# One kernel for two transformer blocks: the output gates' linears move into the recurrences, the modulation weights get a tile of their own in the expert phase

## The chip, the cores and the metric

The kernel runs as one program on 1 core of one Trainium2 chip. The metric is the device time of one execution in microseconds (us). The core's engines are called as in the profile: PE (matrix multiplication), PEld (PE's weight load), DVE (vector), ACT (activations), POOL, and SP, which here only starts DMA transfers.

## What is computed

256 tokens of 1024 channels pass through two blocks, batch 1, everything in fp32.

- Block 1: an adaptive norm (shift, scale and gate of each sub-layer come from `silu(c) @ w_mod + b_mod`), a mixer and a SwiGLU feed-forward. The mixer runs the gated recurrence HGRN2 forward and backward in 4 heads of 128, sums them, and gates: `o_a = rmsnorm(o_f + flip(o_b), g_norm_a) * silu(og)` with `og` one of the columns of the input projection. A second branch is a gated MLP over positions (`u`, `v`); both are merged.
- Block 2, layer 0: chunked gated linear attention (GLA: 4 heads, keys of 128, values of 256, chunks of 64), `o = rmsnorm(o, norm_g) * silu(og)`, then `w_out`. Layer 1: sliding window attention. Behind each stands PEER: a product-key lookup picks 16 of 16384 experts for each of 8 heads of each token, and the experts' `u` and `v` rows are applied. Both layers have their own modulation, and so have the shared keys and values (kv).

## The kernel before

**Linears.** A linear is fp32 made of three matmuls of a reduced 32-bit type (high x high, low x high, high x low: `mm3`, lines 276 to 280). Weights come in halves of 128x1024 (512 KB). For each half, `halves` (lines 257 to 266) starts a DMA on SP's queue into the ring `raw` (line 219; 4 buffers, and more of them, shown as `rawx`, where a stage has room), ACT rounds it to `wh` (line 262), DVE takes the rest as `wl` (line 264; rings of 3 and extras), and PE runs 12 matmuls of 128x512 on it. After each half `pump` adds `s.rate` to a credit, and each full credit calls the background work once.

**Background work: the modulations.** `w_mod` is 1024 x 1024 for each part. A piece (an eighth, 512 KB) is DMAed through the same `raw` ring and multiplied into the activated condition row by one DVE `scalar_tensor_tensor` with a sum (`mod_part`, line 374), which writes over the piece. After eight pieces the part is done (line 378). Where a part is wanted, `need` does what is left at once. Rates: 0.2 in block 1's recurrences, 0.6 from the gates on and in the feed-forward, 0.4 in GLA; in layer 0's PEER 0 in the U phase, 0.45 in the first 36 pairs of the V phase, 0.75 after; in layer 1's V phase 0, then 0.2.

**The order of instructions.** The program is written as one stream, and a scheduler gives each engine its list: it takes what it expects to be ready, in the order of the program where several are. On the chip each engine keeps its list in order and waits for semaphores. Where the scheduler's expectation of a time is off, an engine waits in front of work that is ready.

**The stages that the change touches.**
- Block 1, lines 700 to 875: for `d` in (0, 1) the forget gates f (lines 749 to 753), the products, transposes (L771) and the recurrence. After both: `on`, the sum of squares, `ro`; then the linears og (`w_in` 4, lines 860 to 862, Silu out of PSUM), gu and gv; then `on` times `ro` (L870), times the norm's weights (L872), times og (L873), three passes of 128x512 for each half of the tokens. The transposes of the result are L563.
- GLA, lines 1095 to 1190: q and k linears, k's decayed copy `kd` (L1116, L1117), the transposes of it (L1123), scores, states, outputs (`po` to `on`, line 1172), sums of squares (L1174, L1175), `ro`; then two linears for og (L1181), then the three passes of 128x1024 (L1184, L1186, L1187).
- Feed-forward, lines 960 to 1000: `up0` finishes the first up-block (its transposes are L974), then for each i `up(i + 1)` and the down-projection of block i.
- PEER's `route`, lines 1447 to 1459: the first query linear comes in token-major form; ACT copies it (L1452), PE transposes it (L1455), then the other three query linears run.
- PEER's V phase, lines 1678 to 1735: for each of 64 pairs two halves of `peer_v`, each with 12 matmuls, summed into 4 PSUM banks that stay open. The tile `RO` (1 buffer, 4 KB a partition) serves the gate groups before (line 1630) and the first pair's weights `W01` in this phase; after it, nothing until the next layer.

## Time and profile before

| | |
|---|---|
| median of 3 runs | 2375.7 us (2370.49 to 2376.27) |
| the profiled execution | 2370.87 us, of it the span 2369.1 us |
| mean granted clock of PE | 0.992 of full speed |
| PE busy | 2302.0 us of the span, 97% |
| DVE, ACT busy | 1846.0 us (78%), 1174.3 us (50%) |
| DMA | 475.97 MB, mean 201 GB/s |

The span is the time from the first to the last instruction of the profiled execution; 1.8 us lie around it. An entry such as "idle 2.41 <-DVE w L1117" says that the engine stood still for 2.41 us and that the DVE instruction of line 1117 ended that. Line numbers are those of the kernel before.

### The profile page before, as it was taken

The page shows a single profiled execution, that of the slowest core. Times are in us where ns is not written, and L with a number is a line of the kernel's source. Part 1 is how long each engine was busy: PE and PEld are TensorE (multiplying, and loading weights), DVE is VectorE, ACT ScalarE, POOL GpSimd, SP SyncE. Part 2 cuts the span into 40 slices and gives each one's busy share as a digit, 9 for nine tenths or more (in the row PEclk, how much of TensorE's full clock was granted, in tenths as well). Part 3 has the DMA queues.
Part 4 walks back from the last instruction along what each step waited for, and adds up shares of the span by engine and source line. Part 5 has one row for each costly group of instructions (what it writes and reads, how often), then busy time and mean ns, then how long its engine had stood idle before and what let it go on. Part 6 is the DMA issues. An engine that isn't in the chain of part 4 may idle for free. (4 is left out here: it accounts for less than half of the span.)

```text
span 2369.1 us, 39891 instructions
## 1 busy us (share of the span) xinstructions
PE 2302.0 (97%) x15360; PEld 2043.0 (86%) x15360; DVE 1846.0 (78%) x3502; ACT 1174.3 (50%) x1897; POOL 16.3 (1%) x32
## 2 busy tenths in 40 slices
PE   8999999999999999999999999999999999999998
PEld 6989889976899999997777887589999999888886
DVE  5589887778589989997677877659997999556665
ACT  4464454464445544445454556555454445445543
POOL 0000000000000000000000000000000000000000
PEclk9999999999999999999999999999999999999999
DMA  8537599655445544447778984154554445656773
GB/s 303 177 110 276 174 358 367 219 180 183 144 165 188 162 159 154 150 162 257 252 263 291 346 312 161 45 171 161 179 169 159 153 153 170 189 189 216 240 233 97
DMA packets 130590, 475.97 MB, mean 201 GB/s; under 512 B 15056, under 2 KB 15824, under 8 KB 129120
## 3 DMA queue, kind: packets, MB, share of 16 engines
q1 hardware_dynamic: 130208, 473.41, 59.0%
q8 instruction: 120, 1.97, 0.3%
q14 instruction: 70, 0.57, 0.1%
q0 software_dynamic: 192, 0.02, 0.0%
HBM read 472.30 MB, written 1.07 MB: 200 GB/s over the span
## 5 line engine op out<-in xcount | busy, mean ns | idle before, releaser
L264 DVE TENSOR_TENSOR wl<-raw,wh 128x1024 fp32r<-128x1024 f32 x425 | 517.7, 1221 | 136.7 <-ACT wh L262 135.3
L262 ACT ACTIVATE wh<-raw 128x1024 fp32r<-128x1024 f32 x425 | 448.4, 1056 | 342.9 <-issue 114.3
L1603 PE MATMUL psB<-acth,wh 128*128 128x256 f32 x1776 | 503.6, 284 | 1.6 <-ACT u L1609 1.6
L1605 PE MATMUL psB<-acth,wl 128*128 128x256 f32 x1776 | 500.0, 282 | 0.0
L1604 PE MATMUL psB<-actl,wh 128*128 128x256 f32 x1776 | 499.6, 281 | 0.0
L279 PE MATMUL psA<-wl,acth 128*128 128x512 f32 x880 | 351.3, 399 | 10.7 <-DVE wl L264 10.5
L278 PE MATMUL psA<-wh,acth 128*128 128x512 f32 x880 | 349.9, 398 | 3.5 <-ACT acth L551 2.3
L280 PE MATMUL psA<-wh,actl 128*128 128x512 f32 x880 | 349.2, 397 | 0.5 <-DVE actl L552 0.5
L1603 PEld LDWEIGHTS psB<-acth,wh 128*128 128x128 f32 x1776 | 334.6, 188 | 2.0 <-ACT u L1609 2.0
L1605 PEld LDWEIGHTS psB<-acth,wl 128*128 128x128 f32 x1776 | 334.6, 188 | 0.3 <-DVE wl L264 0.3
L1604 PEld LDWEIGHTS psB<-actl,wh 128*128 128x128 f32 x1776 | 334.7, 188 | 0.0
L279 PEld LDWEIGHTS psA<-wl,acth 128*128 128x128 f32 x880 | 165.9, 189 | 56.2 <-DVE wl L264 16.9
L1697 ACT ACTIVATE acth<-u 128x256 fp32r<-128x256 f32 x240 | 98.5, 416 | 223.1 <-PE psA L279 222.4
L278 PEld LDWEIGHTS psA<-wh,acth 128*128 128x128 f32 x880 | 165.8, 189 | 44.4 <-ACT acth L551 2.4
L280 PEld LDWEIGHTS psA<-wh,actl 128*128 128x128 f32 x880 | 165.6, 188 | 41.0 <-DVE actl L552 0.9
L264 DVE TENSOR_TENSOR wlx<-raw,whx 128x1024 fp32r<-128x1024 f32 x116 | 140.9, 1221 | 38.5 <-ACT whx L262 38.2
L262 ACT ACTIVATE whx<-raw 128x1024 fp32r<-128x1024 f32 x116 | 121.3, 1055 | 74.3 <-PE psB L1604 30.2
L1698 DVE TENSOR_TENSOR actl<-u,acth 128x256 fp32r<-128x256 f32 x240 | 99.7, 422 | 64.3 <-ACT acth L1697 64.3
L262 ACT ACTIVATE wh<-rawx 128x1024 fp32r<-128x1024 f32 x95 | 100.3, 1059 | 86.5 <-PE psB L1604 42.8
L264 DVE TENSOR_TENSOR wl<-rawx,wh 128x1024 fp32r<-128x1024 f32 x95 | 115.9, 1222 | 28.5 <-ACT wh L262 28.0
L262 ACT ACTIVATE whx<-rawx 128x1024 fp32r<-128x1024 f32 x86 | 90.5, 1058 | 83.8 <-PE psB L1604 14.2
L374 DVE SCALAR_TENSOR_TENSOR raw<-raw,L 128x1024 f32<-128x1024 f32 x61 | 74.7, 1224 | 60.7 <-DMA raw<-in_w_kv 30.1
(557 smaller groups left out, 4599.4 us busy)
## 6 DMA issues: line engine op xcount, KB each, us to landing
raw<-in_peer_u SPq DMA_DIRECT2D x212, 512.0 KB, 3.9
raw<-in_peer_v SPq DMA_DIRECT2D x209, 512.0 KB, 4.8
raw<-in_w_m SPq DMA_DIRECT2D x83, 512.0 KB, 5.4
rawx<-in_peer_v SPq DMA_DIRECT2D x47, 512.0 KB, 5.9
rawx<-in_w_m SPq DMA_DIRECT2D x45, 512.0 KB, 6.8
rawx<-in_peer_u SPq DMA_DIRECT2D x44, 512.0 KB, 3.8
raw<-in_w_in SPq DMA_DIRECT2D x27, 512.0 KB, 4.8
rawx<-in_w_up SPq DMA_DIRECT2D x25, 512.0 KB, 8.9
```

Source lines behind the costliest of these rows:

```text
L262: s.queue(nc.scalar.activation(wh, x, AF.Copy))
L264: s.queue(nc.vector.tensor_tensor(wl, x, wh.bitcast(F32), op=OP.subtract))
L278: mm(out, lhsT=lh, rhs=rh, start=start, stop=False)
L279: mm(out, lhsT=lh, rhs=rl, start=False, stop=False)
L280: mm(out, lhsT=ll, rhs=rh, start=False, stop=stop)
L374: s.queue(nc.vector.scalar_tensor_tensor(r, r, 1.0, s.crow, op0=OP.mult, op1=OP.mult, accum_out=m[:, k:k + 1]), 0)
L1603: mm(pu, lhsT=wh[:, sl], rhs=hT[:, k], start=(k == 0), stop=False)
L1604: mm(pu, lhsT=wh[:, sl], rhs=lT[:, k], start=False, stop=False)
L1605: mm(pu, lhsT=wl[:, sl], rhs=hT[:, k], start=False, stop=(k == 7))
L1697: nc.scalar.activation(Wh, W, AF.Copy)
L1698: nc.vector.tensor_tensor(Wl, W, Wh.bitcast(F32), op=OP.subtract)
```

## The change

- The modulation's generator becomes three functions, and while `s.mraw_at` is set, the next piece is DMAed into one tile with the tag `RO` as soon as the piece before is multiplied, instead of through `raw` when its turn comes. It is set in the first 36 pairs of PEER's V phase; of the two layers only layer 0 has pieces there.
- Block 1's og linear moves into the first recurrence (d == 0), behind f, and is kept raw; later ACT makes its Silu in SBUF, and DVE multiplies the norm's weights into it. The three passes become one `scalar_tensor_tensor` per head (8 of 128x128).
- GLA's first og linear moves between `kd` and its transposes, the second stays behind the recurrence; the norm's weights are multiplied into og. The squares are taken by ACT out of PSUM with a sum (8 of 128x256), `rstd` runs for each half of the tokens, and the three passes become 8 `scalar_tensor_tensor` of 128x256.
- Feed-forward: `up(1)` is written ahead of `up0`, and the up-blocks run two ahead of the down-blocks.
- PEER's route: the transposes of the first query linear are written behind the second query linear.

```diff
@@ -157,6 +157,7 @@
+        s.mraw_at = None
...
@@ -179,7 +180,7 @@
-        s.ckey = None
+        s.ckey = s.mnext = None
...
@@ -353,28 +354,43 @@
             nc.vector.tensor_tensor(s.mods["m", part][:, kk * 2:kk * 2 + 2], pt,
                                     b.unsqueeze(2).to_broadcast([128, 2, 2]), op=OP.add)

-    def mod_part(s, key, part):
-
-
-        nc = s.nc
+    def mod_row(s, key):
+
         if s.ckey != (key == "m"):
             s.ckey = key == "m"
             s.crow = s.t(s.crow_at[0], [128, 1024], tag=s.crow_at[1], bufs=1)
             r = 0 if s.ckey else 1
-            nc.sync.dma_start(s.crow, s.a["crow"][r:r + 1, :].to_broadcast([128, 1024]))
-            nc.scalar.activation(s.crow, s.crow, AF.Silu)
-        w = s.a["w_" + key]
+            s.nc.sync.dma_start(s.crow, s.a["crow"][r:r + 1, :].to_broadcast([128, 1024]))
+            s.nc.scalar.activation(s.crow, s.crow, AF.Silu)
+
+    def mod_fetch(s):
+
+        if s.bg and s.mnext is None and s.mraw_at:
+            key, part, k = s.bg[0]
+            s.mnext = s.t(s.mraw_at[0], [128, 1024], tag=s.mraw_at[1], bufs=1)
+            s.nc.sync.dma_start(s.mnext, s.a["w_" + key][part - s.part0[key], k])
+
+    def mod_piece(s):
+
+
+        nc = s.nc
+        key, part, k = s.bg[0]
         gate = part in (2, 5)
-        if gate:
-            m = s.t(s.small, [128, 8], tag="mgate", bufs=2)
-        else:
-            m = s.t(s.early if key == "m" else s.consts, [128, 8])
-        for k in range(8):
-            r = s.raw(w[part - s.part0[key], k])
-            s.queue(nc.vector.scalar_tensor_tensor(r, r, 1.0, s.crow, op0=OP.mult, op1=OP.mult,
-                                                   accum_out=m[:, k:k + 1]), 0)
-            if k < 7:
-                yield
+        s.mod_row(key)
+        s.mod_fetch()
+        r = s.raw(s.a["w_" + key][part - s.part0[key], k]) if s.mnext is None else s.mnext
+        s.mnext = None
+        s.bg.pop(0)
+        if k == 0:
+            if gate:
+                s.mcol = s.t(s.small, [128, 8], tag="mgate", bufs=2)
+            else:
+                s.mcol = s.t(s.early if key == "m" else s.consts, [128, 8])
+        m = s.mcol
+        s.queue(nc.vector.scalar_tensor_tensor(r, r, 1.0, s.crow, op0=OP.mult, op1=OP.mult, accum_out=m[:, k:k + 1]), 0)
+        s.mod_fetch()
+        if k < 7:
+            return
         nc.vector.tensor_tensor(m, m, s.col("mb", 8 * (s.modb0[key] + part), 8), op=OP.add)
         if gate:
             s.uid += 1
@@ -384,19 +400,15 @@
         else:
             s.mods[key, part] = m
         s.done.add((key, part))
-        yield

     def add_mods(s, key, parts):
         for p in parts:
-            s.bg.append(s.mod_part(key, p))
+            s.bg += [(key, p, k) for k in range(8)]

     def pump_n(s, n):
         while n > 0 and s.bg:
-            try:
-                next(s.bg[0])
-                n -= 1
-            except StopIteration:
-                s.bg.pop(0)
+            s.mod_piece()
+            n -= 1

     def pump(s):
         s.credit = getattr(s, "credit", 0.0) + getattr(s, "rate", 0.0)
@@ -708,6 +720,7 @@
                 s.more_mods()
             pb = s.pool("b1b", 1, ctx=c1)
             on = s.t(pb, [128, 2, 4, 128])
+            og = s.t(pb, [128, 2, 512])
             c2 = ExitStack()
             p = s.pool("b1a", 1, ctx=c2)
             w4 = lambda *sh: s.t(p, sh or [128, 4, 256], tag="w4", bufs=8)
@@ -751,6 +764,9 @@
                     nc.scalar.activation(f[:, :, h], bank, AF.Sigmoid)
                     nc.vector.tensor_scalar(f[:, :, h], f[:, :, h], lb1[:, d * 4 + h:d * 4 + h + 1],
                                             lb[:, d * 4 + h:d * 4 + h + 1], op0=OP.mult, op1=OP.add)
+                if d == 0:
+                    for b, y in enumerate(s.lin_nat(w_in, 4, hx, [0, 128])):
+                        nc.scalar.activation(og[:, b], y, AF.Copy)
                 kx, kc = w4(), w4()
                 nc.vector.tensor_scalar(kc, f[:, 1], -1.0, 1.0, op0=OP.mult, op1=OP.add)
                 nc.vector.tensor_scalar(kx, f[:, 0], -1.0, 1.0, op0=OP.mult, op1=OP.add)
@@ -857,20 +873,20 @@
             ro = s.rstd(pb, oss, 8, 128)
             s.rate = s.m2_rate

-            og = s.t(pb, [128, 2, 512])
-            for b, y in enumerate(s.lin_nat(w_in, 4, hx, [0, 128])):
-                nc.scalar.activation(og[:, b], y, AF.Silu)
+            for b in range(2):
+                nc.scalar.activation(og[:, b], og[:, b], AF.Silu)
+                o4 = og[:, b].rearrange("p (h e) -> p h e", h=4)
+                nc.vector.tensor_tensor(o4, o4, gna[:, None, :].to_broadcast([128, 4, 128]), op=OP.mult)
             gu = s.t(pb, [128, 2, 512])
             gv = s.t(pb, [128, 2, 512])
             for n, dst in ((5, gu), (6, gv)):
                 for b, y in enumerate(s.lin_nat(w_in, n, hx, [0, 128])):
                     nc.scalar.activation(dst[:, b], y, AF.Gelu_apprx_tanh)
             for b in range(2):
-                ov = on[:, b]
-                nc.vector.tensor_tensor(ov, ov, ro[:, 4 * b:4 * b + 4].unsqueeze(2).to_broadcast([128, 4, 128]),
-                                        op=OP.mult)
-                nc.vector.tensor_tensor(ov, ov, gna[:, None, :].to_broadcast([128, 4, 128]), op=OP.mult)
-                nc.vector.tensor_tensor(og[:, b], fl(ov), og[:, b], op=OP.mult)
+                for h in range(4):
+                    oh = og[:, b, h * 128:h * 128 + 128]
+                    nc.vector.scalar_tensor_tensor(oh, on[:, b, h], ro[:, 4 * b + h:4 * b + h + 1], oh, op0=OP.mult,
+                                                   op1=OP.mult)
             c2.close()
             p = s.pool("b1c", 1, ctx=c1)
             s.more(c1, 3, 6)
@@ -980,10 +996,12 @@
                 s.mm3(acc[b][n], z[0][:, h, bs], z[1][:, h, bs], w[0][:, sl], w[1][:, sl],
                       i == 0 and h == 0, i == 10 and h == 1)

-            zs = [up0()]
+            z1 = up(1)
+            zs = [up0(), z1]
             acc = [[s.ps("A", [128, 512]) for _ in range(2)] for _ in range(2)]
             for i in range(8):
-                zs.append(up(i + 1))
+                if i < 7:
+                    zs.append(up(i + 2))
                 for h, w in enumerate(s.halves(a["w_down"][i])):
                     for b in range(2):
                         for n in range(2):
@@ -1116,6 +1134,18 @@
                 nc.vector.tensor_tensor(kt[:, sl], bank, e2[:, sl], op=OP.mult)
                 last = nc.vector.tensor_tensor(kd[:, sl], bank, e3[:, sl], op=OP.mult)
             s.hold(last, 2, 2)
+            gn = s.row_bc(pb, "gla_norm")
+            og = s.t(pb, [128, 2, 1024])
+
+            def out_gate(n):
+
+                for b, y in enumerate(s.lin_nat(w, 4 + n, act, [0, 128])):
+                    o = og[:, b, n * 512:n * 512 + 512]
+                    nc.scalar.activation(o, y, AF.Silu)
+                    o2 = o.rearrange("p (h e) -> p h e", h=2)
+                    nc.vector.tensor_tensor(o2, o2, gn[:, None, :].to_broadcast([128, 2, 256]), op=OP.mult)
+
+            out_gate(0)
             kn = w4(128, 2, 4, 128)
             for b in range(2):
                 pt = s.ps("B", [128, 4, 128])
@@ -1152,6 +1182,7 @@
                                                 dv.unsqueeze(2).to_broadcast([128, 2, 256]), op=OP.mult)
                         nc.vector.tensor_tensor(so, pd, so, op=OP.add)
                 st[ch + 1] = sn
+            ros = []
             for b in range(2):
                 for i in range(2):
                     po = s.ps("C", [128, 2, 256])
@@ -1170,21 +1201,15 @@
                                 nc.tensor.matmul(po[64 * r:64 * r + 64, j], lhsT=qt[:, h, ch * 64:ch * 64 + 64],
                                                  rhs=st[ch][:, h], start=False, stop=(j == 1))
                     nc.scalar.activation(on[:, b, 2 * i:2 * i + 2], po, AF.Copy)
-                sq = w4()
-                nc.vector.tensor_tensor(sq, on[:, b], on[:, b], op=OP.mult)
-                nc.vector.tensor_reduce(oss[:, 4 * b:4 * b + 4], sq, axis=AX.X, op=OP.add)
-            ro = s.rstd(pb, oss, 8, 256)
-            gn = s.row_bc(pb, "gla_norm")
-            og = s.t(pb, [128, 2, 1024])
-            for n in range(2):
-                for b, y in enumerate(s.lin_nat(w, 4 + n, act, [0, 128])):
-                    nc.scalar.activation(og[:, b, n * 512:n * 512 + 512], y, AF.Silu)
+                    for j in range(2):
+                        h = 4 * b + 2 * i + j
+                        nc.scalar.activation(po[:, j], po[:, j], AF.Square, accum_out=oss[:, h:h + 1])
+                ros.append(s.rstd(pb, oss[:, 4 * b:4 * b + 4], 4, 256))
+            out_gate(1)
             for b in range(2):
-                ov = on[:, b]
-                nc.vector.tensor_tensor(ov, ov, ro[:, 4 * b:4 * b + 4].unsqueeze(2).to_broadcast([128, 4, 256]),
-                                        op=OP.mult)
-                nc.vector.tensor_tensor(ov, ov, gn[:, None, :].to_broadcast([128, 4, 256]), op=OP.mult)
-                nc.vector.tensor_tensor(og[:, b], fl(ov), og[:, b], op=OP.mult)
+                for h in range(4):
+                    oh = og[:, b, h * 256:h * 256 + 256]
+                    nc.vector.scalar_tensor_tensor(oh, on[:, b, h], ros[b][:, h:h + 1], oh, op0=OP.mult, op1=OP.mult)
             c2.close()
             p = s.pool("glac", 1, ctx=c1)
             s.more(c1, 3, 7)
@@ -1447,16 +1472,19 @@
         i50 = s.t(rp, [128, 50, 16], F16)
         nc.gpsimd.iota(i50, pattern=[[1, 50], [0, 16]], base=0, channel_multiplier=0,
                        allow_small_or_imprecise_dtypes=True)
-        for b, y in enumerate(qfirst):
-            q0 = s.t(rp, [128, 512], tag="sb", bufs=3)
-            nc.scalar.activation(q0, y, AF.Copy)
-            pt = s.ps("A", [128, 4, 128])
-            for j in range(4):
-                nc.tensor.transpose(pt[:, j], q0[:, j * 128:j * 128 + 128], s.ident)
-            nc.scalar.activation(qT[:, 0:4, b * 128:b * 128 + 128], pt, AF.Copy)
+        q0 = []
+        for y in qfirst:
+            q0.append(s.t(rp, [128, 512], tag="sb", bufs=3))
+            nc.scalar.activation(q0[-1], y, AF.Copy)
         for n in range(1, 4):
             for i, bank in enumerate(s.lin_T(a["peer_q"][l], n, act)):
                 nc.scalar.activation(qT[:, 4 * n + 2 * i:4 * n + 2 * i + 2], bank, AF.Copy)
+            if n == 1:
+                for b in range(2):
+                    pt = s.ps("A", [128, 4, 128])
+                    for j in range(4):
+                        nc.tensor.transpose(pt[:, j], q0[b][:, j * 128:j * 128 + 128], s.ident)
+                    nc.scalar.activation(qT[:, 0:4, b * 128:b * 128 + 128], pt, AF.Copy)
         yield
         for b in range(2):
             v16 = s.t(rp, [128, 16, 16], tag="v16", bufs=1)
@@ -1680,6 +1708,7 @@
             acc = [[s.ps("A", [128, 512]) for _ in range(2)] for _ in range(2)]
             W01 = s.t(rl, [128, 2, 2, 256], F32R, tag="RO", bufs=1)
             s.crow_at, s.ckey = (rl, "L"), None
+            s.mraw_at = rl, "RO"
             WH, WL = s.act_tiles()

             made = {}
@@ -1721,6 +1750,7 @@
                     kvp = s.pool("kv", 1, side="right", ctx=s.kvctx) if after == "swa" else None
                     vp = s.pool("peerv", 1, side="right", ctx=vc)
                     s.rate = s.v_rate
+                    s.mraw_at = None
                     s.more(vc, 2, 2, side="right")
                 if at == 58:
                     s.rate = 0.0
```

## Rows read from the trace of the kernel before

**Rows 1.** The page, part 1 (busy time, share, instructions) and lines of part 5.
```profile
PE 2302.0 (97%) x15360; PEld 2043.0 (86%) x15360; DVE 1846.0 (78%) x3502; ACT 1174.3 (50%) x1897; POOL 16.3 (1%) x32
...
L264 DVE TENSOR_TENSOR wl<-raw,wh 128x1024 fp32r<-128x1024 f32 x425 | 517.7, 1221 | 136.7 <-ACT wh L262 135.3
```

**Rows 2.** What the matmuls waited for, whole span: us in total, times, longest.
```profile
PE psA L279 <- DVE wl L264: 10.5, 10, 2.1
...
PE psB L771 <- DVE w L766: 4.2, 1, 4.2
...
PE psB L974 <- DVE z L972: 2.9, 2, 1.5
PE psB L1123 <- DVE w L1117: 2.4, 1, 2.4
```

**Rows 3.** Busy time by stretch: layer 0's V phase, then layer 1's.
```profile
core 0: us, PE busy (x) PEld busy (x) DVE busy (x) ACT busy (x) POOL busy (x), PEclk, DMA share, GB/s
1100.00:1270.00 170.00, 161.01 (x673) 125.81 (x671) 120.53 (x187) 81.31 (x119) 0.88 (x2) 0.99 0.78 260
2000.00:2170.00 170.00, 169.45 (x731) 136.14 (x730) 103.35 (x134) 89.38 (x139) 0.00 (x0) 1.00 0.62 199
```

**Rows 4.** Groups of 1075 to 1290 us: busy, mean ns, idle before and releasers.
```profile
L264 DVE TENSOR_TENSOR wl<-raw,wh 128x1024 fp32r<-128x1024 f32 x70 | 85.5, 1221 | 9.1 <-ACT wh L262 8.6
L262 ACT ACTIVATE wh<-raw 128x1024 fp32r<-128x1024 f32 x70 | 73.9, 1056 | 54.9 <-DMA raw<-in_peer_v 40.2 <-DVE actl L1698 5.1 <-DVE raw L374 4.1
...
L374 DVE SCALAR_TENSOR_TENSOR raw<-raw,L 128x1024 f32<-128x1024 f32 x33 | 40.4, 1226 | 49.7 <-DMA raw<-in_w_kv 30.1 <-DMA raw<-in_w_m 19.5
```

**Rows 5.** Timelines of DVE and SP's queue from 1126 us: start, duration, idle before.
```profile
1126.67 1.23 DVE L374 SCALAR_TENSOR_TENSOR raw<-raw,L 128x1024 f32<-128x1024 f32 x1 [2.54 <-DMA raw<-in_w_kv]
...
1130.00 1.22 DVE L264 TENSOR_TENSOR wl<-raw,wh 128x1024 fp32r<-128x1024 f32 x1 [0.28 <-ACT wh L262]
1132.14 1.23 DVE L374 SCALAR_TENSOR_TENSOR raw<-raw,L 128x1024 f32<-128x1024 f32 x1 [0.92 <-DMA raw<-in_w_kv]
...
1138.08 1.23 DVE L374 SCALAR_TENSOR_TENSOR raw<-raw,L 128x1024 f32<-128x1024 f32 x1 [0.56 <-DMA raw<-in_w_kv]
...
1144.14 1.23 DVE L374 SCALAR_TENSOR_TENSOR raw<-raw,L 128x1024 f32<-128x1024 f32 x1 [1.65 <-DMA raw<-in_w_kv]
...
1127.93 0.33 SPq L219 DMA_DIRECT2D raw<-in_w_kv  x1
1129.41 2.17 SPq L219 DMA_DIRECT2D raw<-in_peer_v  x2
1133.41 0.33 SPq L219 DMA_DIRECT2D raw<-in_w_kv  x1
```

**Rows 6.** Timelines of DVE, SP's queue and ACT, 88 to 98 us.
```profile
91.63 0.55 DVE L752 TENSOR_SCALAR f<-f,u,u 128x512 f32<-128x512 f32 x1 [1.51 <-ACT f L751]
94.81 1.23 DVE L374 SCALAR_TENSOR_TENSOR rawx<-rawx,crow 128x1024 f32<-128x1024 f32 x1 [2.64 <-DMA rawx<-in_w_m]
...
95.96 1.46 DVE L752 TENSOR_SCALAR f<-f,u,u 128x512 f32<-128x512 f32 x3
...
90.14 0.33 SPq L219 DMA_DIRECT2D rawx<-in_w_m  x1
...
90.99 2.72 ACT L751 ACTIVATE f<-psA 128x512 f32<-128x512 f32 x4 [1.29 <-PE psA L314]
```

**Rows 7.** One line's instructions: durations, first and last start (lines 1630, 1642).
```profile
L1630 DVE TENSOR_TENSOR RO<-u,u x64: 1212/1216/1220, 762.7 to 1993.3; 128x2048 f16<-128x2048 f16 x64
...
L1642 PE MATMUL pg<-L,RO x1024: 217/218/237, 868.6 to 1998.3; 128*128 128x128 f16 x171
```

**Rows 8.** PE's gaps on its timeline: line 771, end of block 1's gates, line 1455.
```profile
113.06 1.81 PE L771 MATMUL psB<-u,w 128*128 128x128 f32 x8 [4.23 <-DVE w L766]
...
189.50 0.39 PE L312 MATMUL psA<-acth,wh 128*128 128x256 f32 x1 [1.44 <-ACT wh L262]
...
191.06 1.16 PE L563 MATMUL psB<-u,u 128*128 128x128 f32 x6 [0.82 <-DVE u L873]
...
623.57 0.65 PE L1455 MATMUL psA<-u,sb 128*128 128x128 f32 x4 [1.21 <-ACT sb L1452]
```

**Rows 9.** Windows of 61 us and of 3.3 us (columns as in the windows above).
```profile
124.00:185.00 61.00, 60.99 (x365) 47.34 (x364) 48.44 (x65) 35.51 (x42) 1.74 (x3) 1.00 0.34 109
...
540.00:543.30 3.30, 3.30 (x11) 2.59 (x11) 3.30 (x5) 1.21 (x3) 0.00 (x0) 0.50 0.34 124
```

**Rows 10.** Groups of block 1 and GLA that the edits touch (columns as for groups above).
```profile
L870 DVE TENSOR_TENSOR u<-u,rsy 128x512 f32<-128x512 f32 x2 | 1.3, 687 | 0.0
...
L1187 DVE TENSOR_TENSOR u<-u,u 128x1024 f32<-128x1024 f32 x2 | 2.4, 1222 | 0.0
```

## The prediction, made before the changed kernel was run

> **What bounds the kernel now.** I read the busy times first: PE works in 97% of the span, DVE in 78%, ACT in half [rows 1]. So a DVE or ACT instruction saved is worth nothing by itself; what counts is where PE stands still. The list of what matmuls waited for says where: the largest entry is the last third of a weight half, `wl` (L264), late for L279, 10.5 us in ten waits; then L771 with 4.2, L974 with 2.9, L1123 with 2.4 [rows 2]. The other entries come from stages that the change leaves alone.
>
> Next, the stretch behind the largest entry. Layer 0's V phase and layer 1's run the same matmuls, but in 170 us layer 0 gets 673 through and layer 1 gets 731 [rows 3]. A matmul costs 170 / 731 = 0.233 us there, so the 58 that are missing are 13.5 us; from 1075 to 1290 us about 15 us. That is what the modulation pieces cost, which only layer 0 has. A half is 12 x 0.233 = 2.8 us of PE.
>
> The groups of that stretch show how: 33 pieces (L374) leave DVE idle for 49.7 us in front of their DMA, while ACT waits 40.2 us for halves [rows 4]. Both draw on the same four `raw` tiles. The timelines show the loop: the piece runs for 1.23 us, right behind it SP issues the next piece's transfer (1127.93, 1133.41), and the next piece waits for it [rows 5]. The pieces start at 1126.67, 1132.14, 1138.08, 1144.14: 5.47, 5.94 and 6.06 us apart, 5.8 on average. DVE is in order, so every `wl` behind a waiting piece waits too. With 70 halves for 33 pieces [rows 4], 2.1 halves lie between two pieces, which are 5.9 us of PE: the loop just keeps up, and PE loses only where a landing is late.
>
> **The change part by part.** The sum is made against the profiled execution, 2370.87 us, which is 4.8 below the median of the runs shown.
>
> *A, the pieces in a tile of their own.* Removed: 33 DMAs and their slots from the ring of four, so halves should come earlier and ACT's 40.2 us shrink. Added: nothing; the transfer is issued behind the DVE instruction before, as the trace has it already [rows 5]. The loop (1.26 us from the start of one piece to the issue, 4.2 to 4.8 us to landing, then the next) does not get shorter: 5.85 us is my estimate. What does change is what paces the pieces. Today a piece needs its turn in the ring, so about two halves are ordered between two pieces. With an own tile the loop piece, DMA, piece depends on nothing in PE's stream, and the scheduler may order pieces as early as it thinks that they are ready. That it does so with this very tile the trace shows: the first L1630 into `RO` ran at 762.7, its matmuls at 868.6, 106 us later [rows 7].
>
> And it thinks that a piece is ready sooner than it is. At 94.81 a piece was ordered ahead of three L752 whose inputs ACT had finished by 93.7, the second of them at about 92.4; it waited 2.64 us for a transfer issued at 90.14 [rows 6]. So the expected landing is near 2.2 us, against 4.6 measured. An upper bound is in the V phase: the piece at 1132.14 stands behind a `wl` that ended at 1131.2, 3.3 us after its issue at 1127.93 [rows 5]. The planned loop is then 3.5 to 4.6 us, or 1.3 to 1.65 halves of 2.8 us. I take 4.4 us, 1.6 halves, close to the bound that comes from the same phase. On the chip each loop lasts 5.85 us and feeds PE for 4.4: 33 x 1.45 = 48 us lost, less some 3 that the first buffers (three `wl`) carry, so 45, in place of today's 15: **+30 us**. The ends: at 3.5 us planned 33 x 2.35 = 78, less 15 and 3, gives +60; with the program's spacing of 2.2 halves (6.2 us, over the loop's 5.85) nothing waits and up to 15 us come back, −15. Queued behind each waiting piece on DVE are `wl` and the split of the experts' weights (L1698), and PE and SP's raw transfers wait for those.
>
> The Trainium skill, "DMA: Bandwidth & Descriptors", section "Rules for kernel authors", says to issue a transfer early, compute, and wait late, so that its fixed cost overlaps. By that rule part A would gain; the trace agrees with it only as far as the waiting instruction really stands late in its engine's order, and the rival below prices it.
>
> *B, block 1's og.* 48 matmuls of about 0.233 us, 11 us of PE, move from behind the recurrences into the first. The moved linear brings its four halves, its DMAs on SP, its splits, and pieces at a rate of 0.2 instead of 0.6, so 1.6 pieces fewer run by then; they are made up at the next `need`. The gap before L771, 4.23 us [rows 8], could take this cover. But it comes from DVE, held by pieces waiting for DMA [rows 6], not from PE's lack of ready work alone; og's `wl` would stand in the same DVE order. Bounds: −6 (the gap and the half-clock stretch behind it go) to +6 (144 matmuls of og, gu and gv kept PE at 60.99 of 61.00 us in 124 to 185 [rows 9]; a third of this cover is gone for the second recurrence, and the end of the branch shows). At the end the three passes, six of 0.69 us [rows 10], become eight of a quarter of the size, 0.2 to 0.3 each by my estimate, and ro's dependence stays; the gaps of 1.44 and 0.82 [rows 8] may shrink by 1 to 2 us. I take 0, range −7 to +6.
>
> *C, GLA.* `out_gate(0)` puts 48 matmuls, 11 us, where PE stood 2.41 us for `kd` [rows 2], and where the granted clock was then 0.50 for 3.3 us [rows 9], 1.65 us of lost matmuls. Cover needed is 2.4 us, so both go: −4.1. The three passes of six times 1.22 us on DVE [rows 10] become eight with about the work of two; that tail was hidden but for about 0.8 us. ACT gets eight squares; at half its time idle [rows 1] they hide behind the linears, without that cover some 3 us. The second gate has only 11 us to cover `rstd`. I take −4, range −6 to +1.
>
> *D, feed-forward.* The waits at L974 are 2.9 us [rows 2]. `up(1)` ahead of `up0` covers them if its weights are there; they come from the same DMA stream at the stage's start. −1, range −3 to 0. *E, route.* The transposes waited 1.21 us for ACT's copy [rows 8], and less in layer 1; behind the second linear they don't. −1.5, range −2 to 0.
>
> Sum: +30 + 0 − 4 − 1 − 1.5 = +23.5, so 2394 for a run like the profiled one, and with the 4.8 to the median some **2399, rounded 2400 us**.
>
> **The rivals.** *Faster: the pieces stay at the program's pace.* Then A is worth −13 to −15, since the loop of 5.85 us fits in the 6.2 us of 2.2 halves, and halves have the four tiles to themselves. For it: today's order has 2.1 halves between pieces, and the waits in it are 0.56 to 2.54 us [rows 5]. Against it: that order comes with a ring that both share, and `RO` work was ordered 106 us ahead [rows 7]. With the rest, −14 − 6.5: 2355 at the median, within 2346 to 2366. It decides at a spacing of 5.85 / 2.8 = 2.1 halves. Chance 0.30.
>
> *About even: the planned spacing is near two halves*, 5.5 us against 5.85: 33 x 0.3 = 10 us plus a few for late landings, the same 15 as today; only C to E remain, −6 to +5: 2370 to 2382. For it: the expected landing could be longer beside other transfers (3.3 and more [rows 5]). Chance 0.15.
>
> *Worse than forecast: a loop planned at 3.5 us* (landing as in [rows 6]): +60 − 6.5: 2429. It's in the forecast's own range as its upper end.
>
> **How the numbers follow.** Forecast 0.55 (own range 2383 to 2432), even 0.15, program's pace 0.30. A measurement of this kernel tells 0.3%, 7 us, from no change: 2369 to 2383 is "same". The even case gives 0.11 to same and 0.02 each to the others' sides; the forecast's low edge adds 0.01 to same. So faster 0.32, same 0.12, slower 0.56. For 8 in 10 the range must reach into the faster rival: 2350 to 2432, which leaves out some 0.07 below and 0.05 above.
>
> **What would show it.** Right: in layer 0's V phase pieces 5.8 to 6 us apart with often only one `wl` between them, DVE idle two to three us in front of each for `RO`, ACT's waits for halves gone, many waits of 1 to 2 us of L279 for `wl`, and fewer than 673 matmuls in 170 us while pieces run, then the pace of layer 1 once all 33 are through, some 20 us earlier than now. The waits at L1123 and L1455 are gone, the one at L771 stays. Wrong: two or more `wl` between pieces, pieces that find their data landed, and some 720 matmuls in 170 us. If the block 1 stretch from 92 to 192 is 5 us or more longer or shorter, step B was mis-sized.

## The result, and the profile after

The changed kernel takes 2392.8 us in the median of 8 runs (2382.7 to 2396.1), the kernel before 2374.7 in 8 (2370.5 to 2379.9). The ratio is 1.0067, with an interval of 1.005 to 1.0085: some 16 us slower (from here on, what a kernel gains or loses is worked out from its ratio). The profiled execution of after took 2395.4 us with a span of 2393.6, so it lies at the upper end of its runs, while the one of before lay at the lower end of its own. The difference of the two spans, 24.5 us, is larger than that of the medians.

The busy times of the page answer to [rows 1]:

```profile
PE 2321.0 (97%) x15360; PEld 2055.1 (86%) x15360; DVE 1839.6 (77%) x3519; ACT 1176.8 (49%) x1916; POOL 15.9 (1%) x32
```

The number of matmuls is the same, and PE is busy 19 us longer: most of the loss in this profile is not waiting but matmuls that ran at the lower of the two clock levels, 1.2 instead of 2.4 GHz. The mean granted clock is 0.984, against 0.992 before, which over the two spans is 38 against 19 us of full speed; the waits of the matmuls grew by 5.5 us only (those above 0.15 us, from 57.6 to 63.0). What the matmuls waited for, over the whole span (as in [rows 2]: us in total, times, longest):

```profile
PE psA L88 <- ACT acth L529: 8.3, 6, 1.5
PE psB L575 <- DVE u L888: 5.9, 1, 5.9
PE psB L1415 <- DVE pr L1411: 5.4, 4, 2.1
PE psA L279 <- ACT whx L263: 4.7, 2, 3.1
PE psA L280 <- DVE wl L265: 4.2, 8, 1.0
...
PE psB L787 <- DVE w L782: 2.6, 2, 1.9
...
PE psB L1161 <- ACT w L1154: 2.3, 1, 2.3
PE psB L990 <- DVE z L988: 2.3, 1, 2.3
```

L88's entry was there before, with 6.8 us. L280 is the former L279. Its waits for `wl` fell from 10.5 to 4.2 us, where I had forecast many more. L787 (formerly L771) fell from 4.2 to 2.6, L990 (formerly L974) from 2.9 to 2.3, and L1123's is gone, but the scores just behind it (L1161) now wait 2.3 us. New at the top are the end of block 1's gates (L575), the attention of layer 1 (L1415), and a weight half that came late (L279).

To see where the time goes I set the start of the k-th matmul of one trace beside the k-th of the other; both have 15360. The change of the difference over a stretch is what the stretch cost:

| matmuls | stage | after less before, us |
|---|---|---|
| 0 to 400 | start | +3.0 |
| 400 to 1600 | block 1, recurrences and gates | +6.9 |
| 1600 to 3200 | rest of block 1 | +1.6 |
| 3200 to 4000 | GLA and route, layer 0 | +1.0 |
| 4000 to 8000 | expert U phase, layer 0 | +0.1 |
| 8000 to 9200 | expert V phase, layer 0 | −6.4 |
| 9200 to 9400 | its last halves, kv's weights | +3.2 |
| 9400 to 9800 | attention, layer 1 | +12.1 |
| 9800 to 10000 | route, layer 1 | +5.1 |
| 10000 to 15360 | the rest | −2.1 |

A single pair of profiles is a rough measure: the start, with equal orders, differs by 3.0, and GLA and the route took 3.4 and 3.8 us longer than in the kernel before in two kernels, run below, that leave them as they are. Rows below 4 us say little by themselves.

The stretch that was to lose 30 us gained 6, and the largest loss is in the attention, whose code the change does not touch. The V phase of layer 0, against [rows 3]:

```profile
1100.00:1270.00 170.00, 166.89 (x700) 129.20 (x699) 125.10 (x194) 82.46 (x122) 0.88 (x2) 1.00 0.82 274
```

27 more matmuls than before in 170 us. The timelines of DVE and of SP's queue there answer to [rows 5]:

```profile
1140.60 1.23 DVE L390 SCALAR_TENSOR_TENSOR RO<-RO,L 128x1024 f32<-128x1024 f32 x1 [1.53 <-DMA RO<-in_w_kv]
...
1142.09 1.22 DVE L265 TENSOR_TENSOR wl<-raw,wh 128x1024 fp32r<-128x1024 f32 x1
...
1143.56 1.22 DVE L265 TENSOR_TENSOR wl<-raw,wh 128x1024 fp32r<-128x1024 f32 x1
1146.54 1.23 DVE L390 SCALAR_TENSOR_TENSOR RO<-RO,L 128x1024 f32<-128x1024 f32 x1 [1.76 <-DMA RO<-in_w_kv]
...
1152.27 1.23 DVE L390 SCALAR_TENSOR_TENSOR RO<-RO,L 128x1024 f32<-128x1024 f32 x1 [1.55 <-DMA RO<-in_w_kv]
...
1141.86 0.33 SPq L371 DMA_DIRECT2D RO<-in_w_kv  x1
```

The loop is as forecast: the transfer is issued 1.26 us after the piece starts, the pieces are 5.9 and 5.7 us apart (5.95 on average), and DVE waits in front of each. But two `wl` stand between two pieces, not 1.6 halves; in all 32 intervals of the own tile it is two. Two halves are 5.6 us of PE, so the loop starves PE by 0.3 to 0.4 us a piece. The waits of DVE are as long as before (49.7 us there [rows 4]), and ACT's waits for halves, 40.2 us before, are nearly gone (groups of 1070 to 1320 us):

```profile
L263 ACT ACTIVATE wh<-raw 128x1024 fp32r<-128x1024 f32 x79 | 82.9, 1049 | 13.8 <-DMA raw<-in_peer_v 7.3 <-DVE raw L390 2.0 <-issue 1.4
...
L390 DVE SCALAR_TENSOR_TENSOR RO<-RO,L 128x1024 f32<-128x1024 f32 x33 | 40.4, 1225 | 50.7 <-DMA RO<-in_w_kv 26.2 <-DMA RO<-in_w_m 24.5
```

So some 50 us of idle DVE go with 4.2 us of PE's waits for `wl` here and with 10.5 before: they cost only where the `wl` behind them is the next thing that PE wants.

The attention, in windows over about the same steps: first 1477 to 1515 us of the kernel before, then 1485 to 1530 of the one after (columns as in [rows 3]).

```profile
1477.00:1515.00 38.00, 35.73 (x157) 21.66 (x155) 23.61 (x83) 22.39 (x73) 0.00 (x0) 0.96 0.16 51
```
```profile
1485.00:1530.00 45.00, 39.13 (x146) 23.07 (x145) 21.28 (x75) 19.24 (x60) 0.00 (x0) 0.77 0.16 55
```

The granted clock is 0.77 instead of 0.96. On PE's timeline of after the probabilities' transposes (L1415) stand bare:

```profile
1494.29 0.82 PE L1415 MATMUL psB<-u,pr 128*128 128x128 f32 x4 [2.09 <-DVE pr L1411]
1495.78 0.66 PE L1415 MATMUL psB<-u,pr 128*128 128x128 f32 x2 [0.66 <-DVE pr L1411]
1496.37 1.97 PE L1420 MATMUL psC<-pT,u 128*64 128x512 f32 x2
```

In the kernel before, matmuls of the second query linear ran between these steps. After, 73 matmuls of the two query linears were ordered ahead of the first queries' transposes, 54 before. A linear has 48, so 25 of the second one's were used up instead of 6, and fewer were left to cover the softmax.

My theory at this point: the 33 pieces no longer take their turn in the `raw` ring. The ring's counter, modulo its size, decides whether a weight goes to one of the four standing buffers or to the extra ones of a stage. 33 steps fewer shift the buffers of every weight behind them (by 3 of 6 in the attention), the scheduler then expects other arrival times, and orders the work differently.

### The profile page after: what moved, and what is told of

Same layout as the page of the kernel before. It is cut to its first block, busy times and chain, and to the rows that moved or that the text cites. A ratio compares the mean times of both kernels' runs of the same rounds, so it can differ in the third digit from the quotient of the medians.

```text
span 2393.6 us, 39933 instructions
## 1 busy us (share of the span) xinstructions
PE 2321.0 (97%) x15360; PEld 2055.1 (86%) x15360; DVE 1839.6 (77%) x3519; ACT 1176.8 (49%) x1916; POOL 15.9 (1%) x32
## 5 line engine op out<-in xcount | busy, mean ns | idle before, releaser
L265 DVE TENSOR_TENSOR wl<-raw,wh 128x1024 fp32r<-128x1024 f32 x447 | 544.2, 1220 | 139.5 <-ACT wh L263 138.5
L263 ACT ACTIVATE wh<-raw 128x1024 fp32r<-128x1024 f32 x447 | 470.9, 1054 | 294.5 <-issue 112.7
L280 PE MATMUL psA<-wl,acth 128*128 128x512 f32 x880 | 351.1, 399 | 4.5 <-DVE wl L265 4.2
L279 PE MATMUL psA<-wh,acth 128*128 128x512 f32 x880 | 349.5, 397 | 2.3 <-ACT acth L563 2.3
L280 PEld LDWEIGHTS psA<-wl,acth 128*128 128x128 f32 x880 | 165.6, 188 | 51.9 <-DVE wl L265 13.0
L279 PEld LDWEIGHTS psA<-wh,acth 128*128 128x128 f32 x880 | 165.6, 188 | 42.7 <-ACT acth L563 2.4
L263 ACT ACTIVATE whx<-rawx 128x1024 fp32r<-128x1024 f32 x106 | 111.0, 1055 | 112.5 <-PE psB L575 21.9
L265 DVE TENSOR_TENSOR wlx<-rawx,whx 128x1024 fp32r<-128x1024 f32 x106 | 128.7, 1220 | 44.1 <-ACT whx L263 43.9
L265 DVE TENSOR_TENSOR wlx<-raw,whx 128x1024 fp32r<-128x1024 f32 x96 | 116.1, 1219 | 42.3 <-ACT whx L263 40.4
L263 ACT ACTIVATE whx<-raw 128x1024 fp32r<-128x1024 f32 x96 | 100.2, 1057 | 74.4 <-PE psB L1632 28.2
L263 ACT ACTIVATE wh<-rawx 128x1024 fp32r<-128x1024 f32 x73 | 77.0, 1059 | 70.6 <-PE psB L1632 44.8
L265 DVE TENSOR_TENSOR wl<-rawx,wh 128x1024 fp32r<-128x1024 f32 x73 | 88.9, 1220 | 28.5 <-ACT wh L263 28.4
```

Source lines behind the costliest of these rows:

```text
L263: s.queue(nc.scalar.activation(wh, x, AF.Copy))
L265: s.queue(nc.vector.tensor_tensor(wl, x, wh.bitcast(F32), op=OP.subtract))
L279: mm(out, lhsT=lh, rhs=rh, start=start, stop=False)
L280: mm(out, lhsT=lh, rhs=rl, start=False, stop=False)
```

## The experiments

The kernel before ran again beside each group of kernels, so its median differs a little from one to the next.

**The tile alone.** Of the diff only the modulation's part.

> Only the modulation pieces' own tile, the rest as in the kernel before. Theory (ring phase): the expert phase of layer 0 gets 5 to 7 us shorter, but the 33 pieces no longer take a turn in the raw ring, so the weights behind it fall on other buffers, the scheduler orders the attention of layer 1 differently, with its covering matmuls used up early, and that stage gets 10 to 18 us longer: 4 to 11 us slower than the kernel before. Rival 1 (the prediction's step A): pieces waiting on DVE starve PE in layer 0's expert phase, 20 to 35 us slower, lost between 1075 and 1290 us. Rival 2: the attention's loss comes from another part; then this kernel is 5 to 7 us faster than the kernel before.

Measured: ratio 1.0066 (1.0041 to 1.0091), 2391.1 against 2375.0 us. That is 15.7 us, above the 4 to 11 of the theory. The V phase gained 6.3 us (matmuls 8000 to 8800), the stretch from 8800 to 9600 lost 15.3, the route of layer 1 (9800 to 10000) lost 4.3. The theory had the place of the loss right only in part: the attention (9400 to 9800) lost 6.7, not 10 to 18, and 9.0 were lost ahead of it, in the last halves of `peer_v` (9200 to 9400), where PE stood in one wait (1390 to 1430 us):

```profile
PE psA L279 <- ACT whx L263: 7.5, 1, 7.5
```

The attention's matmuls stand in the order of the full change. Rivals 1 and 2 fall: the tile makes the loss, but not between 1075 and 1290 us.

**The ring's counter kept.** The same, with one line in `mod_piece`:

```diff
+        if s.mnext is not None:
+            s.rings["raw"] += 1
```

> As the run with the modulation tile alone, but each piece that goes through the own tile still advances the ring's counter by one, so that every later weight falls on the buffer that it has in the kernel before. Theory (ring phase): the attention is ordered and timed as before (waits at its probabilities' transposes back to some 2 us, granted clock lower for 3.4 us there only), the expert phase's gain stays: 5 to 7 us faster than the kernel before. Rival 1: starved in the expert phase, 20 us or more slower. Rival 2 (the attention suffers from the pieces being done earlier, not from the ring): as slow as the tile alone, within 2 us.

Measured: 1.0013 (1.0000 to 1.0026), 2379.4 against 2375.0. That is 12 us better than the tile alone, from a counter that only says which buffer a weight falls on; PE's list of instructions is that of the kernel before in every place. Rival 2 falls. But the forecast of a gain was missed too. What the counter returns is the attention and the route: from matmul 9400 to 10000 the tile alone lost 10.9 us, this kernel gained 1.8. The gain of 5.5 us in the V phase is there, but 2.5 are lost by matmul 9200 and 8.7 from there to 9400, around 1410 us, as much as with the tile alone. What happens there shows best on SP's queue, first of the kernel before, then of after:

```profile
1401.04 10.16 SPq L219 DMA_DIRECT2D rawx<-in_peer_v  x6
1411.25 0.42 SPq L219 DMA_DIRECT2D raw<-in_kv_w  x1
```
```profile
1397.80 2.75 SPq L220 DMA_DIRECT2D rawx<-in_peer_v  x2
1407.28 0.33 SPq L220 DMA_DIRECT2D rawx<-in_kv_w  x1
1407.66 1.55 SPq L220 DMA_DIRECT2D rawx<-in_peer_v  x3
1409.30 2.85 SPq L220 DMA_DIRECT2D raw<-in_peer_v  x2
1415.95 0.33 SPq L220 DMA_DIRECT2D rawx<-in_peer_v  x1
```

A transfer of kv's weights, needed only later, stands ahead of six halves of `peer_v` that are needed first. It waits for DVE until 1407, SP issues nothing from 1400.5 to 1407.3, and the halves behind it land late: PE's wait of 3.1 us for `whx` at 1411.6. With the counter kept two of kv's transfers stand ahead, and PE waits for ACT again (SP's queue, then PE's waits of 1390 to 1430 us):

```profile
1404.10 3.94 SPq L220 DMA_DIRECT2D raw<-in_kv_w  x2
1408.10 12.04 SPq L220 DMA_DIRECT2D rawx<-in_peer_v  x6
```
```profile
PE psA L279 <- ACT whx L263: 4.2, 2, 2.8
```

**All but the tile.**

> All of the change but the modulation tile. Theory (ring phase): the attention as in the kernel before; what stays is block 1 (6 to 8 us longer), GLA with the first route (about 3), the second route (up to 5): 6 to 14 us slower than the kernel before, and 5 or more faster than the full change. Prediction's steps B to E: 6.5 us faster than the kernel before. Rival (the attention's loss is not A's): 15 us slower or more.

Measured: 1.0026 (1.0014 to 1.0039), 2383.0 against 2375.0, at the low end of what the theory gave. The steps B to E of the prediction, 6.5 us faster together, fall.

**The full change with the counter kept.**

> The full change, with the ring's counter advanced for each piece of the own tile. Theory (ring phase): 10 to 18 us faster than the full change, so within 6 us of the kernel before. Rival 1 (starved expert phase): as the full change. Rival 2 (other parts upset the attention): within 4 us of the full change.

Measured: 1.0045 (1.0031 to 1.0059), 2387.6, some 5 us faster than the full change. The expectation is missed: in this profile the attention and the route of layer 1 lose nothing any more, where the full change lost 12.1 and 5.1, but the last pairs and the last halves ahead of them (matmuls 8800 to 9400) lost 12.7 us, where the full change lost 3.2. The ring explains a part of the full change's loss, the order of SP's queue, by the next run, another. The 5 us between the two ratios are hardly more than their intervals.

**The order of the transfers.** The tile alone, the counter kept, and from the last pairs of an expert phase to its end each weight transfer follows the one before it in the program:

```diff
         r = s.ring("raw", F32, 4)
-        s.nc.sync.dma_start(r, ap)
+        d = s.nc.sync.dma_start(r, ap)
+        if s.fifo:
+            if s.dlast is not None:
+                s.follow(d, s.dlast)
+            s.dlast = d
         return r
```

> The modulation tile alone, with the ring's counter kept, and the weight transfers held in the order of the program from the last pairs of each expert phase to the end of it, so that no transfer of kv's weights stands on SP's queue ahead of the last halves of peer_v. The order of the matmuls is that of the kernel before in every place. Theory (side effects on later orders): the waits of 3 to 7 us for those halves near 1400 us go, the expert phase's 5 to 7 us stay: 4 to 7 us faster than the kernel before. Rival (the wait is not SP's order but DMA bandwidth or chance): as with the ring kept, 1 to 5 us slower than the kernel before.

Measured: 0.9982 (0.9972 to 0.9992), 2372.7 against 2375.7: faster than the kernel before, by 4.3 us by the ratio. The windows of 1405 to 1425 us with the counter kept, and of 1400 to 1420 with the order held:

```profile
1405.00:1425.00 20.00, 14.34 (x47) 10.24 (x47) 12.84 (x15) 10.15 (x12) 0.00 (x0) 0.83 0.89 308
```
```profile
1400.00:1420.00 20.00, 20.00 (x86) 15.56 (x85) 15.98 (x24) 10.22 (x12) 0.00 (x0) 1.00 0.77 274
```

PE is busy throughout, and the clock stays up, at a DMA rate that is no higher: around 1410 us it was the order in the queue, not bandwidth. The last halves (matmuls 9200 to 9400) lose nothing any more. But the waits are not simply gone: in this profile, that of the slowest of the 11 runs, the pairs ahead of them (8800 to 9200) lose 6.9 us, with 4.9 of waits, where the counter alone lost 2.5; the two other kernels below with the order held lose 7.5 and 6.6 there. Why was not followed up. The gain of 4.3 us is what is left, and rests on the ratio. So counted and ordered the tile gains; without that its side effects cost 20 us more.

The Trainium skill, "DMA: Bandwidth & Descriptors", section "Rules for kernel authors", asks to issue a transfer early and wait late. For the halves of `peer_v` the trace agrees: from 1075 to 1290 us ACT's waits of `wh` for them are 0.2 us, against 40.2 before. For the pieces it does not change: DVE waits 46.7 us for them, against 49.6.

**Block 1's part alone.**

> Block 1's part alone. Theory (cover gone): the matmuls waiting at the end of the gates for the per-head pass stand for 5 to 6 us, the gap ahead of line 771 of the kernel before shrinks by 1 to 3 us, the total is 3 to 7 us slower than the kernel before. Prediction's step B: no change. Rival (the full change's loss there came with the other parts): within 2 us of the kernel before.

Measured: 1.0034 (1.0023 to 1.0044), 2384.5 against 2375.7, 8 us slower: the theory's sign, and a little more than its size. The gap at the end of the gates, 5.9 us, is that of the full change. DVE's timeline of the full change shows what PE waits for there:

```profile
195.11 0.69 DVE L866 TENSOR_TENSOR u<-psB,u 128x512 f32<-128x512 f32 x1 [1.26 <-PE psB L861]
...
195.72 0.68 DVE L872 TENSOR_REDUCE u<-w 128x4 f32<-128x512 f32 x1
...
198.23 0.17 DVE L456 TENSOR_SCALAR rsm<-u 128x8 f32<-128x8 f32 x1
...
200.45 2.19 DVE L888 SCALAR_TENSOR_TENSOR u<-u,rsy,u 128x128 f32<-128x128 f32 x8
```

From the recurrence's last sum (195.1) over the squares, 2.2 us of small steps for the root and the first of eight passes of 0.27 us, to PE's next matmul at 200.9, PE has nothing to do: og's 48 matmuls were used up in the first recurrence. The gap is not the whole loss. The matmuls' waits in block 1 (400 to 1600) grew from 6.5 to 10.8 us, the stretch by 10.9: the rest goes with the clock. In the profile with this part alone the gap lies between 197.3 and 203.1 us, but the clock is at its lower level from 186.4 us, 11 us ahead of it, while PE is busy with the recurrence's last matmuls (columns as in [rows 3]):

```profile
180.00:186.00 6.00, 4.49 (x36) 3.77 (x34) 5.66 (x16) 0.00 (x0) 0.00 (x0) 1.00 0.25 87
187.00:197.00 10.00, 10.00 (x46) 6.08 (x44) 3.72 (x7) 0.00 (x0) 0.00 (x0) 0.50 0.00 1
197.30:203.00 5.70, 0.00 (x0) 0.00 (x0) 5.29 (x18) 0.00 (x0) 0.00 (x0) 0.50 0.24 48
```

**GLA, feed-forward and route together, and each alone.**

> GLA, feed-forward and route, without the modulation tile and without block 1's part. Prediction's steps C, D and E: 6.5 us faster than the kernel before. Theory: 0 to 4 us faster, since after the full change the clock still fell once in GLA and the feed-forward kept a wait of 2.3 us. Rival (moving transposes and linears takes cover from later stages, as in block 1): 2 us slower or more.

Measured: 1.0021 (1.0011 to 1.0032), 2381.9 against 2375.7: 5 us slower, the rival. So each was run alone.

> GLA's part alone. Prediction's step C: 4 us faster than the kernel before. Theory (the cover is only moved): the wait ahead of kd's transposes goes, and the states behind them wait instead, for DVE or ACT, 2 to 4 us: within 2 us of the kernel before.

Measured: 1.0015 (1.0005 to 1.0025), 3.6 us slower, more than the 2 of the theory, which the interval still reaches. PE's waits from 530 to 600 us; in the kernel before it was L1123's 2.4 and 1.9 more:

```profile
PE psA L279 <- DVE wlx L264: 2.0, 1, 2.0
PE psB L1156 <- DVE u L1145: 1.3, 1, 1.3
PE psB L563 <- DVE u L1194: 0.7, 1, 0.7
PE psA L278 <- ACT u L565: 0.7, 1, 0.7
PE psB L1156 <- ACT gS L1160: 0.7, 1, 0.7
PE psA L280 <- DVE u L566: 0.2, 1, 0.2
```

The wait for `kd` is gone, and in its place PE waits for a half and for the states (L1156): 5.6 us of waits instead of 4.3. That the cover is only moved shows here; where the rest of the 3.6 us is lost does not. The wait for `kd` itself was 2.4 to 5.7 us in seven profiles of kernels that leave the order of GLA as it was, so the 2.4 of the profile before is at the low end.

> The feed-forward's part alone. Prediction's step D: 1 us faster (0 to 3). Theory: the two waits at line 974 of 1.45 us become one of about 2 us for the split of the weights and one of 1.5 for the norm's activations, so within 1 us of the kernel before. Rival (the loss of GLA, feed-forward and route together is here): 3 to 5 us slower.

Measured: 1.0008 (0.9998 to 1.0019), not told from no change. The waits ahead of the first up-blocks, 285 to 345 us, against L974's 2.9:

```profile
PE psB L314 <- DVE wlx L264: 2.2, 1, 2.2
PE psA L88 <- ACT acth L517: 1.5, 1, 1.5
PE psB L974 <- DVE z L972: 0.6, 1, 0.6
```

> The route's part alone. Prediction's step E: 1.5 us faster (0 to 2). Theory: the 1.2 us wait of layer 0 goes, in layer 1 nothing changes: 1 us faster. Rival (the loss of GLA, feed-forward and route together is here): 3 to 5 us slower, with waits at the first matmuls behind the second norm.

Measured: 0.9993 (0.9984 to 1.0002), 1.7 us by the ratio, faster, with an interval that just includes none; the wait at L1455 is gone from its profile. The size is the prediction's, as far as it is told from none.

**A version from the parts that pay.** First all but block 1's part, with counter and order kept.

> The full change without block 1's part, with the ring's counter kept and the transfers in the order of the program at the end of each expert phase. Theory: the gains add, 5 to 10 us faster than the kernel before. Rival (the gains are undone by orders further on): within 3 us of the kernel before.

Measured: 1.0009 (0.9999 to 1.002), 2377.3 against 2375.7: the rival. The ratios of the parts alone (−4.3, +3.6, +1.9, −1.7) add up to none. Then the tile with counter and order, and the route's part only.

> The modulation tile with the ring's counter kept and the transfers in the order of the program at the end of the expert phase, and the route's part. Theory: the gains of the two add, 4.3 and 1.8 us: 5 to 7 us faster than the kernel before. Rival (the orders of the two upset one another): no faster than either alone, 1 to 4 us.

Measured: 0.9974 (0.9962 to 0.9985), 2369.1 against 2376.6 us: 6 us faster than the kernel before and some 22 faster than the full change. This fits two gains that add, 4.3 and 1.7; the route's share by itself is not told from none.

## Why the prediction came out as it did

The total was near: 2400 forecast, 2392.8 measured, slower, inside the range. That is luck: the sum behind it was wrong in nearly every term, its +30 in the V phase measured −6, and the loss came from stages that the sum did not have.

- **Step A, +30, failed at "I take 4.4 us, 1.6 halves".** The pieces do run as a loop of their own, at 5.95 us where I had 5.85, with DVE waiting in front of each, as forecast, and slightly ahead of the program's 2.2 halves. But the order leaves two halves between pieces. The ends that I gave for the planned loop, 3.5 to 4.6 us, were too low by the order that came out: two halves are 5.6 us. The L752 case [rows 6], taken as a measure of the expected landing, did not carry over to this stage. What the V phase did is nearest to the rival "about even", two halves and some 9 us still lost of 15, without the few for late landings that it added: −6.4 in the full change's profile, −6.3 with the tile alone, −5.5 with the counter kept.
- **What step A left out.** I counted as removed "33 DMAs and their slots from the ring", and let nothing follow from it but earlier halves. The removed steps shift the ring, and with it the order of work further on: the attention, the queue at kv's weights, the route of layer 1. With the tile alone this cost 22 us, against 6 gained in the V phase: +16. Keeping the count returned 12 us, the attention and the route; holding the queue's order another 7. I had asked which engine gets starved, and not which later stage is ordered from a state that this part leaves behind.
- **Step B, 0 with −7 to +6, measured +8 alone.** The upper end named the cause, "a third of this cover is gone for the second recurrence, and the end of the branch shows". The value taken was the middle. The waits grew by 4.3 us, inside that end, and the lower clock around them adds the rest. I had priced the lower clock where it was in the trace, in step C and in B's lower end, and not in B's upper end, where it would be new.
- **Step C, −4, measured +3.6.** "Cover needed is 2.4 us, so both go" is right for the wait at L1123 and wrong for the sum: the chain behind it (transposes, scores, states) waits as well, and the matmuls moved ahead of it are no longer there. That this is all of the 3.6 us is not shown.
- **Step D, −1, measured +1.9 (−0.5 to +4.5), not clear of none.** The named condition, "if its weights are there", did not hold: the largest wait became one for `wlx`.
- **Step E, −1.5, measured −1.7.** It agrees, the wait is gone as said, but the interval includes none. In the full change layer 1's route lost 5 us; that is the tile's doing, since the tile alone lost 4.3 there, and the route's part alone nothing.
- **The sum itself.** The forecast adds its terms, and the parts don't add. Alone they come to 28 us, together they cost 16. Block 1's part costs 8.1 alone and C to E 5.0, but all but the tile only 6.2. One place shows: where C stands without block 1's part, the matmuls from 3300 to 3900 wait 9.5 to 10.5 us in all in three profiles, with it 5.1 to 5.3 in three; the unchanged GLA waits 7.4 to 10.7. Why block 1's part does this stays open.

The signs forecast for the profile told the terms apart as they should: two `wl` between pieces and 700 matmuls against 673 speak against step A; block 1 longer by 6.9 us (10.9 with its part alone) is the sign named for a mis-sized step B.

## What to carry to other kernels

Cover is one stock: independent matmuls moved ahead to fill one wait are taken from a later one, so price a move by the longest chain that will then run bare, with the lower clock that the trace shows around such stretches. Do not take the costs of parts run alone for their costs together. Where buffers rotate by a counter and a scheduler orders from expected times, taking users out of the ring re-deals everything behind it; keep the count when one part is to be judged, and compare the orders of later stages before blaming the part's own stage. On an in-order DMA queue look for a transfer that is needed late and waits for its buffer ahead of transfers that are needed now.

## What the runs showed of the hardware that was not expected

In block 1 the same order and the same gap of 5.9 us came with very different losses of clock. Around the gap the granted clock was at the lower level for 23.9 us in the profiles of two kernels with block 1's part (this part alone; the full change with the counter kept) and for 10.2 us in two others (the full change; all but the tile). In the first two it fell at 186 us, 11 us ahead of the gap, with no wait of PE above 1.1 us in the 10 us before. In the full change PE stood still from 195.1 us, and the clock fell behind that, at 198.4. The recurrence's last matmuls ran at full clock there (187 to 197 us; the last two of it are the gap):

```profile
187.00:197.00 10.00, 6.97 (x53) 4.36 (x52) 7.83 (x18) 0.00 (x0) 0.00 (x0) 1.00 0.00 1
```

With the clock at 0.50, in the profile of the part alone above, PE needed all of 10 us for 46 of the same matmuls. Block 1 (matmuls 400 to 1600) took 10.9 us longer than in the kernel before in the first two profiles, 6.9 and 5.0 in the others. Why the clock falls early in one profile and late in another is not shown.

The length of such stretches varies between kernels whose orders are equal up to that point: in the first 35 us the 14 profiles had 10 to 17 us at the lower level, up to 3.4 us of time. A single profile of this kernel can therefore not tell 3 us; the ratios above can, where their intervals are narrow enough.
